# Attention projections in another order, one more convolution tap off VectorE, and another end of the kernel

## The chip, the cores and the metric

One core of one Trainium2 chip runs the kernel. The metric is device microseconds (us) of one execution. The engines are TensorE (PE in the rows; its weight loads are PEld), VectorE (DVE), ScalarE (ACT), GpSimd (POOL) and SyncE (SP), which here issues the DMAs.

## The reference

Two transformer-like blocks run one after the other on 512 tokens of width 1024, in fp32. The first block normalizes, projects, mixes the tokens with a state-space part and with a sparse attention, and ends with a feed-forward part. The second block mixes with two recurrent parts and ends with a convolutional feed-forward part and a final norm. What the change touches:

```python
h = rmsnorm(x, norm1_g)                          # first block
hp = h @ w_in                                    # q, the kv streams, gates
q = rmsnorm(q, q_norm_g)                         # each head's 64 values
kc = rmsnorm(compress_blocks(kv[0, 0], ...), k_norm_g[0])   # gelu(flat @ w1) @ w2
vc = compress_blocks(kv[0, 1], ...)
ks, kw = rmsnorm(kv[1, 0], ...), rmsnorm(kv[2, 0], ...)
...
u = dwconv2d(rmsnorm_mod(x) @ w_up, conv_w)      # second block: 3 x 3 taps on 8 x 64 tokens
a, b = split(u)
x = x + g2 * ((silu(a) * b) @ w_down)
out = rmsnorm(x, final_norm_w)
```

## The kernel before

Activations lie with channels on partitions and the 512 tokens along the free axis, in tiles of 128 channels. Every fp32 matrix product is done as three matmuls (`mm3`, lines 210 to 212): activation and weight are each split into a high part (rounded, "H", by ScalarE) and the rest ("L", a subtraction on VectorE or GpSimd), and high x high, low x high and high x low are summed in PSUM. A unit of weights is 128 output channels: `wload` brings it by DMA and splits it into one of three pairs of buffers `wh`, `wl`. `proj` goes through a list of units; a callback takes each finished PSUM tile. With `first=n` the first n units are computed together, with `tail=n` the last n in two halves of the tokens.

PSUM has eight banks, given out by `mmtile` under three tags: four "mm", three "aux" and one "sm". A tile must be read out before its bank is written again. The kernel is written on a layer that sets all the semaphores and that also orders the instructions of each engine: a planner simulates a timeline with costs of its own and takes, among the instructions that are ready in it, the one that comes first in the program. So program order is a priority, and each engine then runs its list in order.

**Attention projections** (`nsa_proj`, line 861). Eight units of `win` are taken in `order`: 4 and 5 are the streams that get compressed, 6 and 7 the keys of the other two branches, 0 to 3 the queries. Each key or query tile is scaled by the token's norm (`qk`, VectorE), squared (ScalarE), and two matmuls with a selector `hsel` (line 895, fp32, one pair for each tile) add the squares of each head into 12 rows of one PSUM tile that stays open through the six tiles. Then the 12 rows are copied, transposed, turned into inverse roots (`root`), transposed back, split (`r12`), and spread by a matmul for each tile (line 915); VectorE multiplies the tile, and `stack` (line 940) copies its halves to `qs` and `ks`. These take the place of the tiles hH and hL, the projections' input, so they can be written only when the last product of `nsa_proj`, the values and gates (`winv`, 96 matmuls into four "mm" tiles), has read it. `compress` (line 976) is a generator with small matmuls (line 1007 and following); after each unit from the third on, one piece of it is put into the program. In `nsa` (line 1075) the compressed values `vcz` enter by a matmul on 64 of the 128 rows (line 1143).

**Second feed-forward part** (`ffn2`, line 1998). `up` takes the units of `wup2`, two for each of 22 pairs. The first 18 units (9 pairs, `lead`) run without any other product, the first four together; then two units alternate with one unit of the down product. `conv_psum` (line 1649) does the nine taps on a unit's PSUM tile: the centre and the tap (-1, 0) on ScalarE, seven taps as multiply-adds on VectorE (line 200), and the addition of the (-1, 0) tap on GpSimd. `gate` multiplies a pair and splits it for the down product. From the fifth unit on GpSimd makes the low part of the weights.

**End.** The last eight units of the down product add to x. The final norm squares the eight tiles, adds them up on VectorE one after the other, sums over partitions by matmuls with ones (line 366), takes the power -1/2 on GpSimd, and spreads the factor (`rdg`, matmul at line 382). `store` makes each output tile with one VectorE instruction, and a DMA takes two tiles. It all runs for each half of the tokens. `between` puts the first half's outputs into the gaps of the second half's norm, in program order.

## Time and profile before

| | |
|---|---|
| runs, median (lowest to highest) | 1656.02 us (1654.74 to 1656.45) |
| profiled execution | 1655.87 us, span 1654.2 us |
| mean granted TensorE clock | 0.973 of full speed |
| busy, TensorE / VectorE / ScalarE / GpSimd | 1571.7 / 1155.2 / 733.0 / 399.6 us |

The span runs from the first to the last instruction. Busy time is the time in which an engine had an instruction in work; its share of the span is 95, 70, 44 and 24%.

### The profile page before, as it was taken

How to read it: one execution, taken by the hardware profiler on the slowest of the kernel's cores; microseconds unless marked ns; L12 is line 12 of the kernel's file. 1: busy time of each engine (PE TensorE's matmuls, PEld its weight loads, DVE VectorE, ACT ScalarE, POOL GpSimd, SP SyncE). 2: the span in 40 equal slices, each digit the busy share in tenths (PEclk: the TensorE clock that was granted, in tenths of full speed). 3: DMA queues.
4: the chain of work that ended last, by engine and by line, in shares of the span. 5: the costliest groups of instructions: out<-in, count | busy, mean ns of one | idle time of the engine just before them, and what ended most of it. 6: DMA issues, size and time to landing. Idle time of an engine off the chain costs nothing.

```text
span 1654.2 us, 22302 instructions
## 1 busy us (share of the span) xinstructions
PE 1571.7 (95%) x8277; PEld 1308.7 (79%) x8277; DVE 1155.2 (70%) x2209; ACT 733.0 (44%) x1286; POOL 399.6 (24%) x355
## 2 busy tenths in 40 slices
PE   7998898899999999999999999989989899999997
PEld 5887676677898888888887888878879788888886
DVE  8988625675769854863538888577868798777755
ACT  4354426553444213352335555556554454343422
POOL 1100203222100000000012222315220566656552
PEclk9999897999999999999999999999999899999998
DMA  5331310003346763733212011111212223233322
GB/s 178 105 96 47 124 59 26 14 20 98 126 166 206 249 218 110 250 124 102 83 64 65 26 39 52 59 52 51 77 52 69 72 94 102 90 102 91 101 86 80
DMA packets 60268, 158.34 MB, mean 96 GB/s; under 512 B 12416, under 2 KB 20352, under 8 KB 60032
## 3 DMA queue, kind: packets, MB, share of 16 engines
q1 hardware_dynamic: 60160, 156.92, 29.9%
q8 instruction: 65, 1.06, 0.3%
q14 instruction: 43, 0.35, 0.1%
HBM read 152.57 MB, written 2.10 MB: 94 GB/s over the span
## 4 chain that ended last, share of the span: by engine, by line
PE 73%; DVE 10%; ACT 5%; issue 2%; POOL 1%; DMA 0%; POOLq 0%; DVEq 0%; ACTq 0%
PE ps_mm L210 21%; PE ps_mm L211 21%; PE ps_mm L212 21%; PE ps_sm L1130 2%; PE ps_mm L1119 1%; DVE caccm L200 1%; DVE wl L191 1%; ACT L188 1%; DVE hgE L191 1%; PE ps_aux L1573 1%; DVE caccf L200 1%; PE ps_aux L1097 1%; ACT wh L188 0%; PE ps_mm L1007 0%; DVE hgl L1486 0%
## 5 line engine op out<-in xcount | busy, mean ns | idle before, releaser
L188 ACT ACTIVATE wh<-raw 128x1024 fp32r<-128x1024 f32 (+3 forms) x234 | 236.7, 1012 | 536.2 <-PE ps_mm L211 415.7
L191 DVE TENSOR_TENSOR wl<-raw,wh 128x1024 fp32r<-128x1024 f32 (+2 forms) x162 | 198.0, 1223 | 115.3 <-ACT wh L188 108.2
L200 DVE SCALAR_TENSOR_TENSOR caccf<-ps_mm,cwf,caccf 128x441 f32<-128x441 f32 (+2 forms) x308 | 206.7, 694 | 34.5 <-ACT ctapf L188 28.8
L191 POOL TENSOR_TENSOR wl<-raw,wh 128x1024 fp32r<-128x1024 f32 (+2 forms) x72 | 159.8, 2221 | 168.0 <-ACT wh L188 167.1
L210 PE MATMUL ps_mm<-h4H,wh 128*128 128x512 f32 (+1 forms) x368 | 137.0, 380 | 7.8 <-DVE caccf L200 7.6
L212 PE MATMUL ps_mm<-h4H,wl 128*128 128x512 f32 (+1 forms) x368 | 138.3, 378 | 0.0
L211 PE MATMUL ps_mm<-h4L,wh 128*128 128x512 f32 (+1 forms) x368 | 138.3, 379 | 0.0
L191 POOL TENSOR_TENSOR rr<-rv,nhalf 128x2 f32<-128x2 f32 x9 | 8.7, 968 | 435.0 <-DVE rv L197 435.0
L210 PE MATMUL ps_mm<-h2H,wh 128*128 128x512 f32 (+1 forms) x280 | 103.8, 372 | 0.0
L212 PE MATMUL ps_mm<-h2H,wl 128*128 128x512 f32 (+1 forms) x280 | 103.6, 371 | 0.0
L211 PE MATMUL ps_mm<-h2L,wh 128*128 128x512 f32 (+1 forms) x280 | 103.6, 371 | 0.0
L210 PE MATMUL ps_mm<-aH,wh 128*128 128x512 f32 (+1 forms) x272 | 102.6, 377 | 0.5 <-DVE x L191 0.5
L212 PE MATMUL ps_mm<-aH,wl 128*128 128x512 f32 (+1 forms) x272 | 102.7, 378 | 0.0
L211 PE MATMUL ps_mm<-aL,wh 128*128 128x512 f32 (+1 forms) x272 | 102.4, 377 | 0.0
L210 PE MATMUL ps_mm<-hH,wh 128*128 128x512 f32 x224 | 89.5, 406 | 9.6 <-ACT hH L188 8.9
L1265 DVE CUSTOM_DVE_ANT_0 msc<-wmod,cB,cols 128x1024 bf16<-128x1024 f32 x64 | 82.0, 1281 | 21.2 <-DMA wmod<-in_wmod 20.8
L211 PE MATMUL ps_mm<-hL,wh 128*128 128x512 f32 x224 | 90.1, 403 | 0.0
L212 PE MATMUL ps_mm<-hH,wl 128*128 128x512 f32 x224 | 89.4, 400 | 0.0
L210 PEld LDWEIGHTS ps_mm<-h4H,wh 128*128 128x128 f32 x368 | 68.7, 190 | 21.1 <-issue 7.7
L211 PEld LDWEIGHTS ps_mm<-h4L,wh 128*128 128x128 f32 x368 | 69.9, 190 | 13.2 <-DVE h4L L200 0.4
L212 PEld LDWEIGHTS ps_mm<-h4H,wl 128*128 128x128 f32 x368 | 69.8, 190 | 13.1
L210 PE MATMUL ps_mm<-faH,wh 128*128 128x512 f32 (+1 forms) x194 | 72.4, 373 | 0.0
(521 smaller groups left out, 4040.9 us busy)
## 6 DMA issues: line engine op xcount, KB each, us to landing
raw<-in_wup SPq DMA_DIRECT2D x76, 512.0 KB, 3.4
wmod<-in_wmod SPq DMA_DIRECT2D x48, 512.0 KB, 4.3
raw<-in_wdn SPq DMA_DIRECT2D x32, 512.0 KB, 3.5
raw<-in_win SPq DMA_DIRECT2D x28, 512.0 KB, 3.4
raw<-in_wout SPq DMA_DIRECT2D x8, 512.0 KB, 3.4
raw<-in_wdn2a SPq DMA_DIRECT2D x8, 512.0 KB, 3.4
raw<-in_wdn2b SPq DMA_DIRECT2D x8, 512.0 KB, 3.4
raw<-in_wdn2c SPq DMA_DIRECT2D x8, 384.0 KB, 3.0
```

The lines of the kernel that those rows point to most:

```text
L188: return self.nc.scalar.activation(o, i, f, **k)
L191: return (e or self.nc.vector).tensor_tensor(o, a, b, op)
L200: return self.nc.vector.scalar_tensor_tensor(o, a, s, b, op0, op1)
L210: mm(ps, wh, xh, start=start, stop=False)
L211: mm(ps, wh, xl, start=False, stop=False)
L212: mm(ps, wl, xh, start=False, stop=stop)
L1097: nc.tensor.matmul(S[:, :n2], self.qs[:, 2 * j + g, c], self.ks[:, 2 * br + g, :n2], start=True, stop=False)
L1119: nc.tensor.transpose(tp[:, 128 * b:128 * b + 128], P[g, i][:, 128 * b:128 * b + 128], self.ident)
L1130: nc.tensor.matmul(O[64 * g:64 * g + 64, 128 * i:128 * i + 128], self.V[:, b, c:c + 64], PT[g][:, 128 * b:128 * b + 128], start=br == 0 an ...
L1265: ins = nc.vector.tensor_tensor_reduce(sc, w, cB[:, c], 1.0, bm[:, m:m + 1], OP.mult, OP.add, acc)
L1573: nc.tensor.matmul(ps[:, j], EE[:, li, 128 * j:128 * j + 128], vw(EE[:, li])[:, j], start=True, stop=True)
```

## The change

The order of the eight attention units becomes 6, 7, 0, 1, 2, 3, 4, 5, and the compression comes into the program as one piece after the stacking, with its PSUM tiles under "aux". Squares are summed three tiles at a time: three selector matmuls write 32 rows each of one PSUM tile, given different column positions of the array; there are two such tiles, so eight transposes where there were four. `vcz` gets zeros in the rows not used, so that its matmul takes all 128 rows. In the feed-forward part the fifth and sixth unit take the banks "aux" and "sm", and the first 18 units have two taps on ScalarE and GpSimd; the taps' order changes. At the end the squares of tiles 0 to 4 are put into the program before the last three units, the eighth tile's squares go to the sum as a second matmul, tiles 6 and 7 of the output are made on ScalarE and GpSimd, and `between` goes away.

```diff
-             pre={}, mid0=None, mid_at=-2):
+             pre={}, mid0=None, mid_at=-2, banks=()):
...
-            ps = self.mmtile()
+            ps = self.mmtile(tag=banks[i - first] if i - first < len(banks) else "mm")
...
-    def sumsq(self, x, tmp, sl, tags=("nsq", "nacc")):
+    def sumsq(self, x, tmp, sl, tags=("nsq", "nacc"), tiles=range(8), acc=None):
         n = sl.stop - sl.start
-        acc = None
-        for k in range(8):
+        for k in tiles:
...
-    def rstd(self, acc, n, width, root=False, between=None):
+    def rstd(self, accs, n, width, root=False):
...
-            self.ss_turn = nc.tensor.matmul(ss[:, j:j + 1], acc[:, 128 * j:128 * j + 128], self.ones[:, :1], start=True,
-                                            stop=True).ins.name
-        between(2)
+            for i, acc in enumerate(accs):
+                self.ss_turn = nc.tensor.matmul(ss[:, j:j + 1], acc[:, 128 * j:128 * j + 128], self.ones[:, :1],
+                                                start=i == 0, stop=i == len(accs) - 1).ins.name
...
-        self.hsel = p.tile([128, 6, 12], F32, name="hsel")
+        self.hsel = p.tile([128, 32], F32, name="hsel")
         e.memset(self.hsel, 0.0)
+        for g in range(2):
+            e.memset(self.hsel[64 * g:64 * g + 64, g:g + 1], 1.0)
...
-        for a in range(6):
-            for g in range(2):
-                e.memset(self.hsel[64 * g:64 * g + 64, a, 2 * a + g:2 * a + g + 1], 1.0)
...
-        ss = self.mmtile((12, T), "aux")
+        slot = (4, 5, 0, 1, 2, 3)
+        sqs, s12 = [], []
...
-        order = (4, 5, 6, 7, 0, 1, 2, 3)
+        order = (6, 7, 0, 1, 2, 3, 4, 5)
...
         def out(i, ps, sl):
             unit(order[i], ps)
-            if i > 1:
-                next(cmp)
...
             self.tt(qk[a], ps, self.rb, OP.mult)
-            sq = qp.tile([128, T], F32, name="sq", tag="sq", bufs=1)
+            sp, tag, bufs = ((qp, "sq", 1), (p, "P03", 2), (p, "P03", 2))[slot.index(a) % 3]
+            sq = sp.tile([128, T], F32, name="sq", tag=tag, bufs=bufs)
             self.act(sq, qk[a], AF.Square)
-            nc.tensor.matmul(ss, self.hsel[:, a], sq, start=a == 4, stop=a == 3)
+            sqs.append(sq)
+            if len(sqs) == 3:
+                ss = self.mmtile((128, T), "aux")
+                for i in range(3):
+                    nc.tensor.matmul(ss[32 * i:32 * i + 32], self.hsel, sqs[i], start=True, stop=True,
+                                     tile_position=(0, 32 * i))
+                sp, tag, bufs = (p, "P03", 2) if s12 else (qp, "s12", 1)
+                t = sp.tile([96, T], F32, name="s12", tag=tag, bufs=bufs)
+                self.act(t, ss[:96])
+                s12.append(t)
+                sqs.clear()
...
-        s12 = qp.tile([12, T], F32, name="s12", tag="s12", bufs=1)
-        self.act(s12, ss)
-        tp = self.mmtile((128, 48), "aux")
-        for i in range(4):
-            nc.tensor.transpose(tp[:, 12 * i:12 * i + 12], s12[:, 128 * i:128 * i + 128], self.ident[:12, :12])
-        r = self.rsqrt(qp, tp, 48, 64, "rn")
+        rr = [qp.tile([128, 4, 2, 6], F32, name="rn" + x) for x in "vrt"]
+        for h in range(2):
+            tp = self.mmtile((128, 4, 3, 32), "aux")
+            for i in range(4):
+                nc.tensor.transpose(tp[:, i], s12[h][:, 128 * i:128 * i + 128], self.ident[:96, :96])
+            self.ts(rr[0][:, :, h].rearrange("p i (s g) -> p i s g", g=2), tp[:, :, :, 0:2], 1.0 / 64, OP.mult, EPS, OP.add)
+        rr = [x.rearrange("p i h s -> p (i h s)") for x in rr]
+        self.root(rr[1], rr[0], rr[2])
+        r = rr[1]
...
-            nc.tensor.matmul(rb, self.hselT[:, a], r12, start=True, stop=True)
+            nc.tensor.matmul(rb, self.hselT[:, slot.index(a)], r12, start=True, stop=True)
             self.stt(qk[a], qk[a], self.col(gcols[a]), rb, OP.mult, OP.mult)
             self.stack(a)
+
+        for _ in cmp:
+            pass
...
-        self.vcz = p.tile([128, 128], F32, name="vcz")
+        self.vcz = p.tile([128, 2, 128], F32, name="vcz")
...
-            hid = self.mmtile((64, 128), "mm")
+            hid = self.mmtile((64, 128), "aux")
...
-            rows = slice(64 * (j % 2), 64 * (j % 2) + 64)
-            nc.tensor.matmul(O, self.vcz[rows], PcT[j // 2][rows], start=False, stop=True, skip_group_check=True)
+            nc.tensor.matmul(O, self.vcz[:, j % 2], PcT[j // 2], start=False, stop=True, skip_group_check=True)
...
-    def conv_psum(self, ps, w, pool, tag, bufs, tbufs):
+    def conv_psum(self, ps, w, pool, tag, bufs, tbufs, n_pool):
...
-        t = pool.tile([128, T], F32, name="ctap" + tag, tag="ctap" + tag, bufs=tbufs)
...
         self.act(acc, ps, scale=w[:, 4:5])
-        self.act(tv[:, 0:7], rv[:, 0:7], scale=w[:, 1:2])
-        for dy, dx in ((1, 0), (0, -1), (0, 1), (-1, -1), (-1, 1), (1, -1), (1, 1)):
+        taps = ((0, -1), (0, 1), (-1, -1), (-1, 1), (1, -1), (1, 1), (1, 0), (-1, 0))
+        late = []
+        for i in range(8 - n_pool, 8):
+            dy, dx = taps[i]
+            c = 3 * (dy + 1) + dx + 1
+            iy = slice(max(0, dy), 8 - max(0, -dy))
+            t = pool.tile([128, T], F32, name="ctap" + tag, tag="ctap" + tag, bufs=tbufs)
+            self.act(g(t)[:, iy], rv[:, iy], scale=w[:, c:c + 1])
+            late.append((slice(max(0, -dy), 8 - max(0, dy)), g(t)[:, iy]))
+        for dy, dx in taps[:8 - n_pool]:
...
-        self.tt(av[:, 1:8], av[:, 1:8], tv[:, 0:7], OP.add, nc.gpsimd)
+        for oy, t in late:
+            self.tt(av[:, oy], av[:, oy], t, OP.add, nc.gpsimd)
...
-                conv[m] = self.conv_psum(ps, cw[:, m // 2 + 22 * (m % 2)], p, "f", 8, 6)
+                conv[m] = self.conv_psum(ps, cw[:, m // 2 + 22 * (m % 2)], p, "f", 8, 6, 2 if m < 2 * lead else 1)
...
             self.proj(I["wup2"][0:2 * lead], hs, up, first=4, pre={3: pre}, halves=True, le=[None] * 4 + [nc.gpsimd] * 18,
+                      banks=("aux", "sm"),
...
+            def factor(sl, acc):
+
+                acc = self.sumsq(self.x, p, sl, tiles=(5, 6), acc=acc)
+                sq = p.tile([128, 256], F32, name="nsq", tag="nsq", bufs=2)
+                self.act(sq, self.x[7][:, sl], AF.Square)
+                return self.rstd([acc, sq], 256, D)[0]
...
             def store(sl, rb):
-                for k in range(8):
-                    if k % 2 == 0:
-                        y = p.tile([128, 2, 256], F32, name="y", tag="faH", bufs=17)
-                    self.tc.keep_in_program_order(
-                        self.stt(y[:, k % 2], self.x[k][:, sl], fin[:, k:k + 1], rb, mul, mul))
-                    if k % 2:
-                        nc.sync.dma_start(self.out[k - 1:k + 1, :, sl].rearrange("k p n -> p k n"), y)
-                    yield
-
-            def between(n):
-                for _ in zip(range(n), s0):
-                    pass
-
-            rb = []
...
-            down("wdn2c", list(range(8)), 16, 6, tail=3, mid=lambda: rb.append(self.norm_factor(self.x, p, h0)))
-            s0 = store(h0, rb[0])
-            r1 = self.rstd(self.sumsq(self.x, p, h1), 256, D, between=between)[0]
-            for _ in store(h1, r1):
-                pass
+
+                y2 = p.tile([128, 2, 256], F32, name="y", tag="faH", bufs=17)
+                for i in range(2):
+                    self.act(y2[:, i], self.x[6 + i][:, sl], scale=fin[:, 6 + i:7 + i])
+                rbs = p.tile([128, 256], F32, name="rbl", tag="rbl", bufs=2)
+                self.act(rbs, rb)
+                for i in range(2):
+                    self.tt(y2[:, i], y2[:, i], rbs, mul, nc.gpsimd)
+                for k in range(0, 6, 2):
+                    y = p.tile([128, 2, 256], F32, name="y", tag="faH", bufs=17)
+                    for i in range(2):
+                        self.stt(y[:, i], self.x[k + i][:, sl], fin[:, k + i:k + i + 1], rb, mul, mul)
+                    nc.sync.dma_start(self.out[k:k + 2, :, sl].rearrange("k p n -> p k n"), y)
+                nc.sync.dma_start(self.out[6:8, :, sl].rearrange("k p n -> p k n"), y2)
+
+
+            early, rb = [], []
+
+            def mid():
+                rb.append(factor(h0, early[0]))
+
+            down("wdn2c", list(range(5)), 16, 6)
+            for i, sl in enumerate((h0, h1)):
+                early.append(self.sumsq(self.x, p, sl, tags=("nsq", f"nacc{i}"), tiles=range(5)))
+            down("wdn2c", [5, 6, 7], 16, 6, tail=3, mid=mid)
+            r1 = factor(h1, early[1])
+            store(h0, rb[0])
+            store(h1, r1)
```

## Rows read from the trace of the kernel before

**Rows 1.** Waits of TensorE, whole span: us in total, times, longest.

```profile
PE ps_mm L210 <- DVE caccf L200: 7.6, 1, 7.6
```

**Rows 2.** Busy time by stages: stretch, length; us busy (instructions) by engine; PEclk; DMA share, GB/s.

```profile
262.00:272.00 10.00, 5.76 (x15) 3.46 (x14) 9.66 (x19) 9.68 (x16) 2.06 (x3) 0.72 0.20 52
...
1286.00:1300.00 14.00, 6.44 (x46) 5.97 (x45) 11.77 (x19) 9.05 (x13) 8.25 (x4) 0.78 0.36 112
...
1304.00:1376.00 72.00, 72.00 (x319) 59.63 (x319) 64.63 (x103) 35.19 (x53) 46.47 (x27) 1.00 0.28 88
```

**Rows 3.** Timeline of TensorE, 1298 to 1305: start, us, instruction, count, idle before.

```profile
1298.49 0.76 PE L210 MATMUL ps_mm<-h4H,wh 128*128 128x512 f32 x1 [7.56 <-DVE caccf L200]
...
1304.11 0.39 PE L211 MATMUL ps_mm<-h4L,wh 128*128 128x512 f32 x1
1304.33 0.39 PE L212 MATMUL ps_mm<-h4H,wl 128*128 128x512 f32 x1
```

**Rows 4.** Timelines of VectorE and of GpSimd, same place.

```profile
1288.16 17.26 DVE L200 SCALAR_TENSOR_TENSOR caccf<-ps_mm,cwf,caccf 128x448 f32<-128x448 f32 x28 [5.75 <-ACT ctapf L188]
...
1287.10 4.75 POOL L191 TENSOR_TENSOR wl<-raw,wh 128x1024 fp32r<-128x1024 f32 x2 [14.87 <-ACT wh L188]
```

**Rows 5.** Groups by line, 1304 to 1376: count | busy us, mean ns | idle before.

```profile
L188 ACT ACTIVATE ctapf<-ps_mm,cwf 128x448 f32<-128x448 f32 x13 | 8.1, 625 | 0.0
...
L200 DVE SCALAR_TENSOR_TENSOR caccf<-ps_mm,cwf,caccf 128x441 f32<-128x441 f32 (+2 forms) x89 | 58.4, 692 | 7.4 <-ACT ctapf L188 6.4
...
L191 POOL TENSOR_TENSOR wl<-raw,wh 128x1024 fp32r<-128x1024 f32 x13 | 31.3, 2407 | 12.6 <-ACT wh L188 12.1
L191 POOL TENSOR_TENSOR caccf<-caccf,ctapf 128x448 f32<-128x448 f32 x14 | 16.2, 1156 | 15.9 <-DVE caccf L200 15.9
```

**Rows 6.** The page's 40 slices, TensorE: busy tenths.

```profile
PE   7998898899999999999999999989989899999997
```

**Rows 7.** Timeline of TensorE, attention: compression, one sum pair, and an attention product.

```profile
199.61 4.12 PE L1007 MATMUL ps_mm<-cw,cD 128*64 128x128 f32 x32
...
204.09 1.03 PE L895 MATMUL ps_aux<-sq,hsel 128*12 128x512 f32 x2
...
293.49 1.74 PE L1130 MATMUL ps_sm<-PT,V 128*64 128x128 f32 x26
```

**Rows 8.** Timelines of TensorE, VectorE and ScalarE, end of the projections.

```profile
257.24 0.29 PE L212 MATMUL ps_mm<-wh,hL 128*128 128x280 f32 x1
...
257.88 0.68 DVE L191 TENSOR_TENSOR r<-ps_aux,r 12x512 fp32r<-12x512 f32 x1 [4.40 <-ACT r L188]
...
254.81 0.48 ACT L188 ACTIVATE V<-ps_mm,rr 128x256 f32<-128x256 f32 x1 [0.16 <-PE ps_mm L212]
...
258.63 0.26 ACT L188 ACTIVATE gat<-ps_mm,rr 128x24 f32<-128x24 f32 x1
...
261.71 1.28 ACT L188 ACTIVATE qs<-qk 64x512 fp32r<-64x512 f32 x2 [0.93 <-DVE qk L200]
...
268.19 3.90 ACT L188 ACTIVATE qs<-qk 64x512 fp32r<-64x512 f32 x6
```

**Rows 9.** Timelines of ScalarE, TensorE, GpSimd and VectorE, end of the kernel.

```profile
1642.29 0.42 ACT L188 ACTIVATE nsq<-x 128x256 f32<-128x256 f32 x1 [0.42 <-DVE nacc L191]
...
1643.46 0.58 PE L366 MATMUL ps_sm<-ones,nacc 128*128 128x1 f32 x4 [1.63 <-DVE nacc L191]
...
1645.52 1.22 PE L382 MATMUL ps_aux<-rdg,ones 128*128 128x256 f32 x2 [1.49 <-DVE rdg L191]
...
1644.31 0.69 POOL L191 TENSOR_TENSOR rr<-rv,nhalf 128x2 f32<-128x2 f32 x1 [3.69 <-DVE rv L197]
...
1645.38 4.79 DVE L200 SCALAR_TENSOR_TENSOR y<-x,cols,ps_aux 128x256 f32<-128x256 f32 x12
```

**Rows 10.** Timelines of VectorE and GpSimd, before the end.

```profile
1617.14 1.64 DVE L191 TENSOR_TENSOR nacc<-nsq 128x256 f32<-128x256 f32 x1 [0.48 <-ACT nsq L188]
...
1616.65 1.85 POOL L191 TENSOR_TENSOR wl<-raw,wh 128x768 fp32r<-128x768 f32 x1 [2.27 <-ACT wh L188]
```

More of the change, by code (lines that the diff above doesn't have):

```diff
@@ L326, in norm_factor @@
     def norm_factor(self, x, tmp, sl):
-        return self.rstd(self.sumsq(x, tmp, sl), sl.stop - sl.start, D)[0]
+        return self.rstd([self.sumsq(x, tmp, sl)], sl.stop - sl.start, D)[0]
     def norm(self, x, g, h, tmp, shift, sl, tag="nt", rb=None, bufs=2):
@@ L355, in split_scaled @@
             self.stt(L[:, k, sl], x[k][:, sl], g[:, k:k + 1], H[:, k, sl].bitcast(F32), OP.mult, OP.subtract)
-    def rstd(self, acc, n, width, root=False, between=None):
+    def rstd(self, accs, n, width, root=False):
         nc = self.nc
-        pin = self.tc.keep_in_program_order if between else lambda i: i
-        between = between or (lambda n: None)
         nb = n // 128
@@ L365, in rstd @@
         for j in range(nb):
-            self.ss_turn = nc.tensor.matmul(ss[:, j:j + 1], acc[:, 128 * j:128 * j + 128], self.ones[:, :1], start=True,
-                                            stop=True).ins.name
-        between(2)
+            for i, acc in enumerate(accs):
+                self.ss_turn = nc.tensor.matmul(ss[:, j:j + 1], acc[:, 128 * j:128 * j + 128], self.ones[:, :1],
+                                                start=i == 0, stop=i == len(accs) - 1).ins.name
         v = self.sm.tile([128, 4], F32, name="rv", tag="rv", bufs=2)
-        pin(self.ts(v[:, :nb], ss[:, :nb], 1.0 / width, OP.mult, EPS, OP.add))
+        self.ts(v[:, :nb], ss[:, :nb], 1.0 / width, OP.mult, EPS, OP.add)
         r = self.sm.tile([128, 4], F32, name="rr", tag="rr", bufs=2)
@@ L377, in rstd @@
         dg = self.sm.tile([128, 512], F32, name="rdg", tag="rdg", bufs=1)
-        between(2)
-        pin(self.tt(dg[:, :n].rearrange("p (b t) -> p b t", b=nb), self.ident[:, None, :].to_broadcast([128, nb, 128]),
-                    r[:, :nb, None].to_broadcast([128, nb, 128]), OP.mult))
+        self.tt(dg[:, :n].rearrange("p (b t) -> p b t", b=nb), self.ident[:, None, :].to_broadcast([128, nb, 128]),
+                r[:, :nb, None].to_broadcast([128, nb, 128]), OP.mult)
         rb = self.mmtile((128, 512), "mm" if root else "aux")
         nc.tensor.matmul(rb[:, :n], self.ones, dg[:, :n], start=True, stop=True)
-        between(8)
         return rb[:, :n], r
@@ L602, in norm @@
         def norm():
-            r, self.rt = self.rstd(self.sumsq(xs, hp, full, ("yg", "glus")), T, D, root=True)
+            r, self.rt = self.rstd([self.sumsq(xs, hp, full, ("yg", "glus"))], T, D, root=True)
             self.act(self.rb, r)
@@ L958, in stack @@
             self.tt(L, t[r], H[r].bitcast(F32), OP.subtract, self.nc.gpsimd if a in (2,3) else None)
-    def rsqrt(self, p, ss, n, width, nm):
-        v, r, t = (p.tile([128, n], F32, name=nm + x) for x in "vrt")
-        self.ts(v, ss, 1.0 / width, OP.mult, EPS, OP.add)
-        self.root(r, v, t)
-        return r
     def root(self, r, v, t):
@@ L1013, in compress @@
         for m in (4, 5):
-            tp = self.mmtile((128, 64), "mm")
+            tp = self.mmtile((128, 64), "aux")
             nc.tensor.transpose(tp, hids[m - 4], self.ident[:64, :64])
@@ L1019, in compress @@
             yield
-        kp = self.mmtile((64, 64), "mm")
+        kp = self.mmtile((64, 64), "aux")
         nc.tensor.matmul(kp, hTs[0][:, 0], w2[:, :64], start=True, stop=True)
@@ L1031, in compress @@
         yield
-        vp = self.mmtile((128, 64), "mm")
+        vp = self.mmtile((128, 64), "aux")
         nc.tensor.matmul(vp, hTs[1].rearrange("p a b -> p (a b)"), w2[:, 64:], start=True, stop=True)
@@ L1035, in compress @@
             s = slice(32 * b, 32 * b + 32)
-            self.act(self.vcz[s, 64 * (b % 2):64 * (b % 2) + 64], vp[s])
-        tp = self.mmtile((128, 64), "mm")
+            self.act(self.vcz[s, b // 2, 64 * (b % 2):64 * (b % 2) + 64], vp[s])
+        tp = self.mmtile((128, 64), "aux")
         nc.tensor.transpose(tp, kz, self.ident[:64, :64])
@@ L1647, in conv @@
         return acc
-    def conv_psum(self, ps, w, pool, tag, bufs, tbufs):
+    def conv_psum(self, ps, w, pool, tag, bufs, tbufs, n_pool):
         nc = self.nc
         acc = pool.tile([128, T], F32, name="cacc" + tag, tag="cacc" + tag, bufs=bufs)
-        t = pool.tile([128, T], F32, name="ctap" + tag, tag="ctap" + tag, bufs=tbufs)
         g = lambda a: a.rearrange("p (y x) -> p y x", x=64)
-        av, rv, tv = g(acc), g(ps), g(t)
+        av, rv = g(acc), g(ps)
         self.act(acc, ps, scale=w[:, 4:5])
-        self.act(tv[:, 0:7], rv[:, 0:7], scale=w[:, 1:2])
-        for dy, dx in ((1, 0), (0, -1), (0, 1), (-1, -1), (-1, 1), (1, -1), (1, 1)):
+        taps = ((0, -1), (0, 1), (-1, -1), (-1, 1), (1, -1), (1, 1), (1, 0), (-1, 0))
[8 more added lines that the diff above has]
+        for dy, dx in taps[:8 - n_pool]:
             c = 3 * (dy + 1) + dx + 1
@@ L2063, in between @@
-            def between(n):
-                for _ in zip(range(n), s0):
-                    pass
-            rb = []
-            h0, h1 = slice(0, 256), slice(256, 512)
-            down("wdn2c", list(range(8)), 16, 6, tail=3, mid=lambda: rb.append(self.norm_factor(self.x, p, h0)))
-            s0 = store(h0, rb[0])
-            r1 = self.rstd(self.sumsq(self.x, p, h1), 256, D, between=between)[0]
-            for _ in store(h1, r1):
-                pass
+            h0, h1 = slice(0, 256), slice(256, 512)
```

## The prediction

> **What bounds the kernel now.** The share of busy time says TensorE, 95% (the table). What matters is the remaining 82.5 us of its span (1654.2 less 1571.7), so I read the waits of TensorE first. They are many and short; one of 7.6 us stands out, in the second feed-forward part, where the first matmul of a new unit waits for VectorE's convolution to give a PSUM bank back [rows 1]. Second, the table by stages: three stretches touched by the change have an idle TensorE, 1286 to 1300 (6.4 of 14 us busy, granted clock 0.78), 262 to 272 (5.8 of 10 us, clock 0.72) and the end; the stage from 1304 to 1376, between, has TensorE busy for all of its 72 us [rows 2]. Third, the timeline of each of the three, since a gain counts only if TensorE is dense from there to the next stop. The time compared is the profiled execution's 1655.87 us: 1654.2 of span and 1.67 around it, which I leave as it is. The median of the runs, 1656.02, is 0.01% away, so no correction.
>
> **Feed-forward, start.** The first four units are computed together and hold all four "mm" banks. TensorE stands for 7.56 us until 1298.49, and then it runs slowly: thirteen matmuls from 1298.49 to 1304.11 take 5.62 us, where the pitch of the next pieces is 0.22 to 0.23 (1304.11 to 1304.33), 2.95 us for thirteen [rows 3]. That is 2.67 us for the low clock level (1.2 GHz; 2.4 is the other), which follows the idle time. The change gives the fifth and sixth unit the banks "aux" and "sm". A unit is 8 x 3 matmuls, 24 x 0.227 = 5.44 us, so TensorE has 10.9 us of work from about 1290.9 to 1301.8 before it asks for an "mm" bank. Are the weights there? Two units' low halves leave GpSimd from 1287.10 to 1291.85, one as 1290.9 is reached, the other with 4 us to spare [rows 4]. Is the first bank back by 1301.8? In the trace it came at 1298.49, inside 28 convolution taps that VectorE runs in 17.26 us from 1288.16 [rows 4]; with 24 taps they end at 1288.16 + 24 x 0.616 = 1302.9, the first unit's before that. So the stall goes with its clock: 7.56 + 2.67 = **10.2 us**. Bounds: 10.2 and, if the planner interleaves the taps so that the first unit's end among the last at 1302.9, or the second's are later still, about 5.
>
> What is late next? One tap more per unit for the first 18 units goes to ScalarE (0.625 us) and GpSimd (1.156), and VectorE loses one of 0.69 [rows 5]. These 18 units are dense on TensorE at 5.5 us a unit (13 units in 72 us) [rows 2, 5]. VectorE was at 64.63 of 72, 4.97 a unit; it falls to 4.3. That is worth nothing in itself, since it was not the limit from 1304 on. ScalarE goes from 2.7 to 3.3 a unit, off the path. GpSimd goes from 46.47 of 72, 3.6 a unit, to 2.407 + 2 x 1.156 = 4.72, still below 5.44: cost 0, hidden under the matmuls, with 0.7 us a unit to spare. Behind a GpSimd addition that waits for its taps stands the split of a later unit's weights, and TensorE waits for that; if the cover goes, the price is the last rival. For later units only the order of the taps is changed: 0. From 1304 TensorE's slices stay at 9 tenths or more to the last but one [rows 6], so the 10.2 reaches the end.
>
> **Projections.** From the glu on, TensorE is dense until the last V matmul starts at 257.24 [rows 8]. In that stretch six pairs of sum-of-squares matmuls take 1.03 us each, about 1.1 with the matmul behind, which starts slower [rows 7]: 6.6. The new ones are two groups of three pairs on 32 columns each. Side by side a group is about 1.03, one after the other 3.1, and I find nothing that puts a group beyond these two. The nearest row: 26 half-width instructions of 128 columns in 1.74 us, 0.067 each, against 32 of full output layout, 4.12 us, 0.129 each [rows 7]: neighbours on different columns run nearly twice as fast, so I take 1.1 a group, 2.2 together; saved 4.4 (0.4 if serial). Added ahead of the last V matmul: six broadcasts of the factors, which ran after it, 6 x 0.227 = 1.4; four more transposes and one more interruption, about 0.7. Net 2.3: the V products end at 255.2 instead of 257.5. The compression's matmuls, two runs of 4.12, stay ahead of that end (they come before V in the program): moved, not removed, 0.
>
> After them the old order waits: the factors are split on VectorE at 257.88, the scaling follows, and the first copy to the stacked heads on ScalarE at 261.71 [rows 8]. The copies need scaled q and k and the h tiles free (the stacked tiles take their place). With q and k first, the scaling is over during the last two units, so the copies start when h is free, 255.4: 6.3 us earlier. From there ScalarE is the path: 16 copies until 272.09, then a table load and the exponentials [rows 8]. What is late next is ScalarE itself: the evacuations of V and the gates, 254.81 to 258.89, lay in its idle time [rows 8] and now partly fall into the copies. They start 2.7 us before the end of V (257.5), so up to 1.4 are left; I take 0.8. The memsets of the stacked keys on GpSimd and the compression's small ScalarE work move with the same wait for h, or lie beside the 12 us of V matmuls: 0. Sum **5.5 us**. Bounds: the norm's transposes and broadcasts now stand inside the running units on TensorE's in-order queue, and behind each of them a unit's matmuls; if their inputs come late by a microsecond or two at each of four places, the gain is gone: -1. The other end is 14 (first rival). The zero-padded V of the compressed branch keeps 512 streamed columns: 0. SP's loads of compression weights move back by six units, behind the unit weights that are needed first: 0.
>
> **The end.** Old chain after the last residual: the last square waits 0.42 for a buffer (1642.29), an addition follows, TensorE sums from 1643.46, GpSimd's power is 1644.31 to 1645.00, the factor's broadcast is 1645.52 to 1646.74, and VectorE has twelve products left at 1645.38, to 1650.17, 0.40 each, eight of them behind the broadcast [rows 9]. New: no buffer wait and no last addition, less two more sums, about 0.5 earlier; six products behind the broadcast instead of eight, 0.8; the other two go to ScalarE and GpSimd beside them. Sum **1.3 us**; 0.5 to 2.5.
>
> One row speaks against the new GpSimd products: an addition of two SBUF tiles on VectorE took 1.64 us beside a GpSimd product that ran 1616.65 to 1618.50, where twelve products of the same 256 columns run at 0.40 each [rows 9, 10]. The Trainium skill (GPSIMD Engine Reference, Specifications) says that GpSimd shares its SBUF interfaces with VectorE, in contention with instructions that have two SBUF inputs. The trace agrees. By it, the diagonal of the second half's factor (two SBUF inputs) can be held by a product of the first half, up to 0.7 us, and the end would give 0.6 instead of 1.3.
>
> Together 10.2 + 5.5 + 1.3 = 17.0: 1655.87 - 17.0 = **1638.9 us**.
>
> **Rivals.** (1) The compression's 8.2 us of matmuls fall behind V, into the time when TensorE waits for ScalarE's copies, and h is free 8.2 earlier. For it: TensorE has 4.2 us idle from 262 to 272 [rows 2] and the matmuls no longer use the "mm" banks that V holds. Against: in program order they stand before V and their inputs are ready early in V's 12 us. 1655.87 - 25.2 = 1630.7.
> (2) The start gives half: the fifth and sixth units run at once, but the banks come late, as the 24 taps end at 1302.9 and not at 1301.8, and each stop brings slow matmuls; 5 for the start and 2 for the projections, 1.3 for the end: 1647.6.
> (3) It doesn't do what it says: the planner's order puts new stops into the units (norm) and the start, and nothing or 3 us remain: 1653 to 1657.
> (4) GpSimd's queue becomes the bound of the first 18 units. It had 28.5 us of waits in those 72 us, 2.2 a unit, for ScalarE's copies and for VectorE's taps in turn [rows 5]. With 4.72 of work, and the waits as long as now, a unit takes 6.9 and TensorE follows it through three weight buffers: 1.46 x 14 units (the fifth to the eighteenth) = 20.5 lost, 1659.4, slower. It decides from 17.0 / 14 = 1.2 us a unit. Against: most of those waits are slack of an engine that is early, and VectorE ends its taps sooner.
>
> **Numbers.** Forecast 0.53, (1) 0.12, (2) 0.20, (3) 0.08, (4) 0.07. The forecast's own range is 1634 to 1644; towards (1) the low end is 1630, and to hold most of (2) the high end is 1650, which leaves out (3), (4) and a little of (1). This kernel's time can be told from no change at about 0.2%, 3.3 us: faster is the first three, 0.85; the same 0.08; slower 0.07.
>
> **What would show it.** Start: the wait for a convolution's bank is gone, the stretch 1291 to 1304 (shifted) is busy at full clock, and no wait of TensorE for weights comes in the units after. Projections: the six-instruction groups take about 1 us, the V products end 2.3 us earlier, the first copy starts within 1 us of them, the exponentials 5 to 6 us earlier. End: the last product about 1.3 us nearer to the last matmul. Wrong would be a new TensorE wait in the units, or the first unit's taps ending after TensorE asks.

## The result, and the profile after

The changed kernel takes 1637.19 us (median of 4 runs, 1636.85 to 1637.37) against 1656.13 for the kernel before on the same chip: ratio 0.9887, 95% interval 0.987 to 0.9904, 18.9 us less. The prediction was 1638.9, 17.0 less. The total came out nearly as forecast; its three terms did not.

To see the terms, I cut every trace at five marks on TensorE: **A**, the first product of `ysH` behind the wait of 7.49 us for ScalarE; the first product of `mH` (the merge behind the attention); the first of `h4H` (second feed-forward part); the first of `faH`; the last of `faH`/`faL`. The table holds the start of A and the differences of the starts, in us, with the kernels of the experiments below; each row is one execution. "Stretch 1" is projections and attention, "stretch 3" the first feed-forward units.

| kernel | A | 1: to `mH` | 2: to `h4H` | 3: to `faH` | 4: to last | to end | span |
|---|---|---|---|---|---|---|---|
| before | 175.92 | 239.56 | 850.30 | 122.42 | 252.92 | 13.08 | 1654.2 |
| changed | 175.06 | 229.88 | 849.96 | 113.79 | 253.36 | 12.75 | 1634.8 |
| changed, again (e9) | 175.06 | 229.63 | 849.95 | 113.73 | 253.37 | 12.76 | 1634.5 |
| e1 banks | 173.65 | 238.67 | 852.32 | 121.46 | 252.92 | 12.98 | 1652.0 |
| e2 taps | 175.88 | 240.10 | 849.62 | 119.09 | 252.92 | 13.09 | 1650.7 |
| e5 banks and taps | 177.77 | 240.24 | 849.50 | 113.75 | 252.91 | 13.03 | 1647.2 |
| e3 projections | 174.57 | 230.25 | 849.97 | 122.48 | 252.92 | 12.41 | 1642.6 |
| e4 end | 174.83 | 241.21 | 849.59 | 122.45 | 253.36 | 13.46 | 1654.9 |
| e6 sums adjacent | 176.34 | 226.82 | 850.19 | 113.73 | 253.36 | 12.76 | 1633.2 |
| e7 compression early | 173.22 | 227.21 | 848.93 | 113.74 | 253.37 | 12.63 | 1629.1 |
| e8 compression late | 175.56 | 244.81 | 849.03 | 113.76 | 253.37 | 13.37 | 1649.9 |
| e10 end ordered | 177.74 | 229.80 | 850.07 | 113.72 | 253.37 | 12.20 | 1636.9 |
| e11 adjacent, early | 175.35 | 224.15 | 849.42 | 113.78 | 253.37 | 12.63 | 1628.7 |
| e12 all | 175.15 | 226.74 | 849.32 | 113.76 | 253.37 | 12.06 | 1630.4 |

Stretch 3 repeats to 0.1 us between kernels with the same code there. Stretch 1 spreads by 2.5 over the five kernels that have the old projections (238.67 to 241.21, mean 239.96) and by 0.6 over the four with the new ones as changed (229.63 to 230.25, mean 229.89). So the change gives 10.1 in the projections (predicted 5.5), 8.7 in the feed-forward start (122.45 to 113.75; predicted 10.2), and takes 0.4 in stretch 4, with nothing sure from there to the end (12.41 to 13.09 with the old end, 12.63 to 13.46 with the changed one; predicted gain 1.3).

Stages of the changed kernel, which answer to [rows 2] (it runs ahead by some 11 us at the feed-forward part):

```profile
250.00:262.00 12.00, 8.56 (x57) 7.90 (x58) 9.59 (x9) 9.97 (x18) 9.05 (x7) 0.87 0.46 131
262.00:272.00 10.00, 8.24 (x32) 7.02 (x31) 3.51 (x16) 6.27 (x21) 3.31 (x4) 0.50 0.00 0
1275.00:1288.00 13.00, 12.27 (x74) 10.64 (x73) 10.08 (x17) 9.97 (x15) 9.15 (x5) 1.00 0.33 105
1288.00:1300.00 12.00, 12.00 (x54) 9.95 (x53) 6.79 (x12) 6.85 (x11) 12.00 (x9) 1.00 0.30 107
1300.00:1372.00 72.00, 71.63 (x316) 58.91 (x315) 67.98 (x107) 45.17 (x72) 64.86 (x43) 1.00 0.30 95
```

The hole at the feed-forward start is closed, at granted clock 1.00. GpSimd rises to 64.86 of 72 and TensorE is still busy for 71.63. TensorE's waits there, against the 7.6 of [rows 1]:

```profile
PE ps_sm L212 <- POOL wl L191: 0.7, 1, 0.7
PE ps_mm L210 <- DVE caccf L200: 0.4, 1, 0.4
```

Timeline of TensorE around the end of the projections, for [rows 7, 8] (start, us, instruction, idle before). L895 are the sums, L1012 the compression, L1020 and L1043 its transposes, L1102 the first score:

```profile
198.85 1.04 PE L895 MATMUL ps_aux<-sq,hsel 128*32 128x512 f32 x2
...
218.75 1.05 PE L895 MATMUL ps_aux<-sq,hsel 128*32 128x512 f32 x4
...
250.42 4.13 PE L1012 MATMUL ps_aux<-cw,cD 128*64 128x128 f32 x32 [0.57 <-DVE qk L200]
...
259.99 0.36 PE L1020 MATMUL ps_aux<-ident,chs 64*128 64x64 f32 x1 [2.48 <-ACT chs L188]
...
267.16 0.34 PE L1043 MATMUL ps_aux<-ident,kz 64*128 64x64 f32 x1 [1.40 <-DVE kz L200]
267.42 0.58 PE L1102 MATMUL ps_aux<-ks,qs 128*128 128x256 f32 x1
```

ScalarE there: the first copy to the stacked heads, the last group of them, and the first exponential.

```profile
246.41 1.29 ACT L188 ACTIVATE qs<-qk 64x512 fp32r<-64x512 f32 x2
...
254.47 3.88 ACT L188 ACTIVATE qs<-qk 64x512 fp32r<-64x512 f32 x6
...
269.06 0.40 ACT L188 ACTIVATE P<-P,mn 128x128 f32<-128x128 f32 x1
```

The V products end at 246.39 (257.53 before), the compression now follows them, and the sums stand in five places of the units, not two. The end, against [rows 9]: VectorE runs six products of the first half ahead of the second half's variance `rv`, and the last six start behind ScalarE's copy.

```profile
1623.22 2.44 DVE L200 SCALAR_TENSOR_TENSOR y<-x,cols,ps_aux 128x256 f32<-128x256 f32 x6 [0.36 <-ACT rbl L188]
1625.57 0.15 DVE L197 TENSOR_SCALAR rv<-ps_sm 128x2 f32<-128x2 f32 x1
1626.53 0.42 DVE L191 TENSOR_TENSOR rdg<-ident,rr 128x256 f32<-128x256 f32 x1 [0.81 <-POOL rr L191]
1628.16 2.44 DVE L200 SCALAR_TENSOR_TENSOR y<-x,cols,ps_aux 128x256 f32<-128x256 f32 x6 [1.21 <-ACT rbl L188]
```

### The profile page after: what moved, and what is told of

Its sections match the earlier page's. It is cut to its first block, busy times and chain, and to the rows that moved or that the text cites. A ratio compares the mean times of both kernels' runs of the same rounds, so it can differ in the third digit from the quotient of the medians.

```text
span 1634.8 us, 22321 instructions
## 1 busy us (share of the span) xinstructions
PE 1557.2 (95%) x8289; PEld 1302.4 (80%) x8289; DVE 1144.3 (70%) x2186; ACT 745.0 (46%) x1311; POOL 423.7 (26%) x367
## 3 DMA queue, kind: packets, MB, share of 16 engines
q8 instruction: 65, 1.06, 0.3%
## 4 chain that ended last, share of the span: by engine, by line
PE 72%; DVE 10%; ACT 5%; issue 2%; POOL 1%; DMA 0%; DVEq 0%; ACTq 0%
PE ps_mm L210 20%; PE ps_mm L212 20%; PE ps_mm L211 20%; PE ps_sm L1135 2%; DVE wl L191 1%; PE ps_mm L1124 1%; DVE caccm L200 1%; ACT L188 1%; DVE hgE L191 1%; PE ps_aux L1102 1%; ACT wh L188 1%; PE ps_aux L1104 1%; PE ps_aux L1577 1%; DVE caccf L200 1%; DVE hgl L1490 0%
## 5 line engine op out<-in xcount | busy, mean ns | idle before, releaser
L200 DVE SCALAR_TENSOR_TENSOR caccf<-ps_mm,cwf,caccf 128x441 f32<-128x441 f32 (+2 forms) x278 | 188.5, 695 | 30.9 <-ACT ctapf L188 24.7
L212 PE MATMUL ps_mm<-h4H,wl 128*128 128x512 f32 (+1 forms) x352 | 131.2, 375 | 0.0
L211 PE MATMUL ps_mm<-h4L,wh 128*128 128x512 f32 (+1 forms) x352 | 131.1, 375 | 0.0
L210 PE MATMUL ps_mm<-h4H,wh 128*128 128x512 f32 (+1 forms) x352 | 129.7, 377 | 0.6 <-DVE caccf L200 0.4
L211 PEld LDWEIGHTS ps_mm<-h4L,wh 128*128 128x128 f32 x352 | 66.2, 188 | 12.5 <-DVE h4L L200 0.4
L212 PEld LDWEIGHTS ps_mm<-h4H,wl 128*128 128x128 f32 x352 | 66.2, 188 | 12.2
L210 PEld LDWEIGHTS ps_mm<-h4H,wh 128*128 128x128 f32 x352 | 65.0, 188 | 13.3 <-issue 0.8
```

Source lines behind the costliest of these rows:

```text
L200: return self.nc.vector.scalar_tensor_tensor(o, a, s, b, op0, op1)
L210: mm(ps, wh, xh, start=start, stop=False)
L211: mm(ps, wh, xl, start=False, stop=False)
L212: mm(ps, wl, xh, start=False, stop=stop)
```

## The experiments

**Each part alone on the kernel before (e1 to e4), then two together (e5).** Each is the kernel before with only those lines of the diff. e1:

```diff
+                      banks=("aux", "sm"),
```

> One part alone on the kernel before: the fifth and sixth feed-forward units get the banks "aux" and "sm"; the taps stay at 28 in VectorE for the first four units. The prediction's sizes: the stall of 7.56 us and the slow matmuls of 2.67 us go together, but the taps end later than with 24, 28 x 0.616 = 17.26 us after their start, at the time when TensorE asks for an "mm" bank, so 6 to 10 us gained, 1646 to 1650. Theory B, from the trace of the changed kernel (its feed-forward stretch is 8.4 us shorter and keeps 0.73 and 0.37 us of waits): the banks are all of it, 7 to 9 us, 1647 to 1649. Theory C, the banks only move the stall behind the sixth unit because the taps set the pace: under 4 us, 1652 or more.

Measured: 1653.81 us, ratio 0.9998 (0.9989 to 1.0008); stretch 3 is 121.46, 1.0 less. Theory C. TensorE's waits from 1270 to 1400 (us in total, times, longest):

```profile
PE ps_mm L210 <- DVE caccf L200: 6.2, 2, 4.9
```

and the second of the two stops in TensorE's timeline:

```profile
1329.72 0.76 PE L210 MATMUL ps_mm<-h4H,wh 128*128 128x512 f32 x1 [4.88 <-DVE caccf L200]
```

The stop of [rows 3] is not removed; most of it moves 31 us on, and slow matmuls follow it again (granted clock 0.82 from 1330 to 1340). VectorE is busy for all of the 10 us ahead of it. e2:

```diff
-                conv[m] = self.conv_psum(ps, cw[:, m // 2 + 22 * (m % 2)], p, "f", 8, 6)
+                conv[m] = self.conv_psum(ps, cw[:, m // 2 + 22 * (m % 2)], p, "f", 8, 6, 2 if m < 2 * lead else 1)
```

> One part alone on the kernel before: a second tap of the first 18 units on ScalarE and GpSimd, and the new order of taps; no new banks, projections and end as before. The prediction's price of this part is 0 where TensorE is dense; alone, where the stall is still there, four taps fewer in VectorE before the first bank is free bring 0.6 to 2.5 us: 1653.5 to 1655.5. The rival that GpSimd's queue becomes the bound of these units: 1.2 us a unit or more, 1670 or so.

Measured: 1652.12, ratio 0.998 (0.9971 to 0.9989), stretch 3 3.3 less. The one wait for a bank falls from 7.6 to this:

```profile
PE ps_mm L210 <- DVE caccf L200: 4.0, 1, 4.0
```

1.4 us more than the expected bounds, and no sign of GpSimd as the bound. e5, both:

> The two feed-forward parts together on the kernel before (new banks, and the second tap of the first 18 units off VectorE); projections and end as before. Alone they gave 0.4 to 1.7 us (banks) and 3.4 us (taps). Theory A, the two add up: 1651 to 1652. Theory B, each lacks the other: with the banks alone the stall of 7.56 us only moves, to 4.9 us some 31 us later, because VectorE gains on TensorE too slowly to give the banks back in time; with fewer taps it does. Then both together bring the 8.4 us that the feed-forward stretch of the changed kernel is shorter: 1646 to 1648.

Measured: 1647.11, ratio 0.9947 (0.9932 to 0.9963), stretch 3 113.75: 8.7 less, where the parts alone sum to 4.3. Theory B: the banks let TensorE go on, and only the shorter taps keep VectorE's backlog from stopping it again.

e3, the projections alone:

```diff
-        order = (4, 5, 6, 7, 0, 1, 2, 3)
+        order = (6, 7, 0, 1, 2, 3, 4, 5)
```

> One part alone on the kernel before: the projections (keys and queries first, compressed streams last, sums of squares in two groups, compression in "aux" banks, zero-padded V of the compressed branch). Prediction: 5.5 us, 1650.6. Theory B, from the trace of the changed kernel, where the attention starts 10 us sooner and the compression's matmuls lie behind the V products: 10 to 11 us, 1645 to 1646, with the stretch of the glu ahead of it 0.9 us shorter.

Measured: 1642.79, ratio 0.9929 (0.9914 to 0.9943); stretch 1 230.25, 9.7 under the mean of the old ones. By the stage, theory B's size; the median is 12.7 under the kernel before's (1655.5), more than either theory (four runs, 1641.15 to 1644.53). The part of theory B on the glu fell, since A differs as much between kernels with one order there. e4, the end alone:

```diff
-            r1 = self.rstd(self.sumsq(self.x, p, h1), 256, D, between=between)[0]
+            r1 = factor(h1, early[1])
+            store(h0, rb[0])
+            store(h1, r1)
```

> One part alone on the kernel before: the end (first five tiles' squares summed earlier, last square straight into TensorE's sum, two of eight products on ScalarE and GpSimd, no order pinned between the two halves). Prediction: 1.3 us, 1654.8, bounds 0.5 to 2.5. Theory B, from the trace of the changed kernel (12.5 us from the last matmul of the residuals to the end, 12.8 before): 0.3 us, 1655.8, because six products of the first half run on VectorE ahead of the second half's factor.

Measured: 1656.86, ratio 1.0009 (0.9999 to 1.0018): no gain, at most a loss. Stretch 4 is 0.44 longer, as in every kernel with the new end; the trace shows eight one-column sums of the first half inside it, where the old end had four; no run changes these alone.

**Sums adjacent (e6)**, on the changed kernel:

```diff
-            self.act(sq, qk[a], AF.Square)
+            last = self.act(sq, qk[a], AF.Square).ins.name
...
+                    if i < 2:
+                        self.tc.add_manual_dep(ins.ins, last, NOSYNC, reason="group")
```

> The changed kernel, but the first two sums of squares of each group are ordered behind the third square, so that the three of a group follow one another on TensorE (in the changed kernel five interruptions of 1.04 to 1.05 us hold the six). The prediction's step (side by side a group of three takes about 1.05 us): two interruptions instead of five, 3.1 us sooner at the last V matmul, and 2 to 3 us in all, 1634 to 1635. The rival, that they run one after the other however they are placed: the group takes 3.1 us, no gain, 1637; the factors come some microseconds later, which could cost up to 1: 1638.

Measured: 1632.32, ratio 0.9861 (0.9845 to 0.9877), a little more gain than expected; stretch 1 226.82, 3.1 less. Timeline of TensorE:

```profile
205.57 1.06 PE L895 MATMUL ps_aux<-sq,hsel 128*32 128x512 f32 x6
...
223.12 1.06 PE L895 MATMUL ps_aux<-sq,hsel 128*32 128x512 f32 x6
```

Six instructions on three column groups take 1.06 us, two on one took 1.04. The prediction's price for a group was right; the changed kernel's order does not make the groups.

**Compression ahead of the end of V (e7)**, the place that the prediction gave it; all its PSUM tiles go to "sm", of which the cut shows one:

```diff
         self.proj([I["win"][4 + m] for m in order], hs, out)
+        for _ in cmp:
+            pass
...
-            hid = self.mmtile((64, 128), "aux")
+            hid = self.mmtile((64, 128), "sm")
```

> The changed kernel, but the compression is traced directly behind the units (in bank "sm"), so that its matmuls fall ahead of the end of the V products, as the prediction had it. Theory A, that the compression fell behind V is what made the gain in the attention larger than predicted: V ends 8 to 9 us later (255), and the time is 4 to 5 us longer, 1641 to 1642. Theory B, the order of the compression only decides where the wait lies: the copies end 8 us later but the exponentials follow them directly (267 to 268.5, against 269.06), and the time stays at 1636 to 1638.

Measured: 1632.97, ratio 0.9862 (0.9845 to 0.9878). Both theories expected too long a time: stretch 1 is 227.21, 2.7 less than the changed kernel's. V ends at 254.73, the first copy is at 254.70, the last copy ends at 264.96 and the first exponential is here:

```profile
267.70 0.40 ACT L188 ACTIVATE P<-P,mn 128x128 f32<-128x128 f32 x1
```

From A that is 94.48 us, against 94.00 in the changed kernel (269.06 less 175.06): no gain up to there. The gain lies behind it. TensorE's waits, changed kernel from 190 to 420:

```profile
PE ps_aux L1142 <- DVE cX L191: 4.8, 1, 4.8
PE ps_aux L1020 <- ACT chs L188: 2.8, 2, 2.5
PE ps_aux L1043 <- DVE kz L200: 1.4, 1, 1.4
PE ps_aux L1102 <- DVE mn L1108: 1.1, 3, 0.5
```

and with the compression early:

```profile
PE ps_aux L1102 <- DVE mn L1108: 4.6, 6, 2.0
PE ps_sm L1043 <- ACT vcz L188: 2.4, 1, 2.4
PE ps_aux L1102 <- ACT ks L188: 1.3, 2, 0.9
...
PE ps_aux L1060 <- ACT kcbd L188: 0.8, 1, 0.8
```

The wait for `cX` (the compressed branch's weights, in TensorE's queue ahead of the second branch) is gone; so is the one for the gelu. The kernel before has the wait for `cX` too:

```profile
PE ps_aux L1137 <- DVE cX L191: 4.8, 1, 4.8
```

From 285 to 305 TensorE is busy for 18.70 of 20 us, against 15.19 (A is 1.84 earlier in e7; from 283.16 to 303.16, as far behind A as the other, it is 18.70 too).

**Compression after the first branch (e8):**

```diff
                 if j == 0 and br == 1:
+                    for _ in self.cmp:
+                        pass
                     X = self.nsa_cmp(p)
```

> The changed kernel, but the compression is traced after the first branch of the first head pair, directly ahead of its use. Theory A, the chain through the compression (gelu behind ScalarE's 16 copies, 10.7 us from the last copy at 258.35 to the first exponential at 269.06) bounds the start of the attention: the first exponential comes at 259.7 to 261, two more table loads cost 2.6, and 3 to 6 us are gained, 1631 to 1634. Theory B, behind the first exponentials the same work of ScalarE and VectorE has to be done, and the compression's matmuls and table loads now stand in it: no gain or a loss of up to 3, 1637 to 1640.

Measured: 1652.29, ratio 0.9987 (0.9972 to 1.0001): 15 us slower than the changed kernel, worse than either theory, though the first exponential came at 260.30. TensorE's waits:

```profile
PE ps_mm L1125 <- DVE P L196: 7.7, 4, 4.5
PE ps_aux L1103 <- DVE mn L1109: 5.4, 7, 3.3
PE ps_aux L1011 <- DMA cw<-in_ck: 2.1, 2, 1.1
```

From 262 to 285 VectorE is busy for 6.26 us and ScalarE for 7.29 of 23: the compression's chain stands alone there, its weights loaded late into buffers that it shares with the attention. Being first at the exponentials is worth nothing by itself.

**The changed kernel again (e9, no edit), and the end in another order (e10):**

```diff
-            r1 = factor(h1, early[1])
-            store(h0, rb[0])
-            store(h1, r1)
+            s0 = store(h0, rb[0][0])
...
+            r1 = factor(h1, early[1], between, "mm")
...
+            rc = self.mmtile((128, 512), copy)
+            nc.tensor.matmul(rc[:, :n], self.ones, dg[:, :n], start=True, stop=True)
```

> The changed kernel itself, beside the three below on the same chip, so that differences of a few microseconds between them can be read. Both theories: 1637, ratio to the kernel before 0.9887 within its interval.

> The changed kernel with another order at the end: the second half's variance and diagonal on VectorE go ahead of four of the first half's six products, GpSimd's power ahead of its products, and the broadcast factor is written to a second bank that ScalarE reads, so that VectorE need not wait for ScalarE's copy. Theory A, the end gave nothing because of the two stops in VectorE (the variance 1.1 us late behind six products, then 1.21 us behind ScalarE's copy): 1.5 to 2.3 us less than the changed kernel. Theory B, the chain of square, sum, power, diagonal and broadcast with the write to memory sets the end, whatever VectorE does beside it: 0 to 0.7 us less.

Measured: e9 1636.35, ratio 0.9882 (0.9863 to 0.9902); e10 1636.70, 0.9883 (0.9865 to 0.9901). Theory B. VectorE's two stops are gone:

```profile
1626.94 0.86 DVE L200 SCALAR_TENSOR_TENSOR y<-x,cols,ps_aux 128x256 f32<-128x256 f32 x2
1627.84 0.94 DVE L191 TENSOR_TENSOR rdg<-ident,rr 128x256 f32<-128x256 f32 x1
1628.70 3.31 DVE L200 SCALAR_TENSOR_TENSOR y<-x,cols,ps_aux 128x256 f32<-128x256 f32 x8
```

The last product ends 7.31 us behind the last `fa` start (1632.01 less 1624.70), against 8.55 in the changed kernel (1630.60 less 1622.05), but the kernel's end comes only 0.55 sooner (12.20, 12.75). The rest goes into writing: what the DMA engines moved in 40 slices from 1618 to 1660, first changed, then e10:

```profile
GB/s 0 0 0 0 0 0 95 342 341 220 0 201 338 350 110 0 8 8 0 0 0 0 0 0 0 0 0 0 0 0 0 0 0 0 0 0 0 0 0 0
```

```profile
GB/s 0 0 0 0 0 0 0 0 55 195 248 32 343 344 331 351 99 0 8 8 0 0 0 0 0 0 0 0 0 0 0 0 0 0 0 0 0 0 0 0
```

Eight transfers of 256 KB at 330 to 350 GB/s; with the first half's products later, more of them crowd behind the last.

**Together (e11), and with a transposition moved and the new end (e12).** e12's own edit traces the transposed `kz` ahead of the `vp` product.

> The changed kernel with the sums of squares adjacent and the compression ahead of the end of the V products. Alone the spans were 1.6 and 5.7 us shorter than the changed kernel's. Theory A, the two add up (one moves the end of V, the other what follows it): span 1627 to 1628. Theory B, behind V both work on the same wait (first exponentials), and the smaller is lost: span 1629.

> The two together, with the new order at the end, and with the transposed compressed key traced ahead of the compressed value (with the compression early TensorE waited 2.42 us for its bank, held until ScalarE had copied the compressed value, and 0.83 us for its copy). Theory A: both waits go and the end gives 1.5 to 2.3 us, span 1623 to 1625. Theory B, only what bounds the first exponentials counts, ScalarE's copies: 0 to 1 for the transposition and 0 to 0.7 for the end, span 1626.5 to 1628.

Measured: e11 1630.43, ratio 0.9845 (0.9829 to 0.986), span 1628.7. It is the fastest, on one chip with e9 5.9 us under it. In stretch 1 the two add up: 224.15, 5.7 under the 229.89, where e6 gave 3.1 and e7 2.7 (theory A; in the spans the unequal A hides it). e12 1633.24, 0.9863: slower than e11. Both theories fell. TensorE's waits from 228 to 420:

```profile
PE ps_aux L1113 <- DVE mn L1119: 4.1, 5, 2.8
PE ps_aux L1153 <- DVE w L1124: 3.0, 1, 3.0
PE ps_sm L1052 <- ACT kcbd L188: 1.8, 1, 1.8
```

The wait of 2.4 is shortened to 1.8, and the stop ahead of the `cX` transposes (L1153) is back with 3.0. VectorE ends the last product with `cX` at 292.82 in e12 and at 288.70 in e11, where it follows its inputs directly. In e12 two score operations, the biases of the next heads and a product `gt` that waits for TensorE are ahead of it in VectorE's queue, and then it takes 2.26 us instead of 1.23. e12's VectorE and GpSimd:

```profile
289.95 0.69 DVE L191 TENSOR_TENSOR gt<-gt,ps_mm 128x512 f32<-128x512 f32 x1 [0.47 <-PE ps_mm L212]
290.56 2.26 DVE L191 TENSOR_TENSOR cX<-cX,csm 128x1024 f32<-128x1024 f32 x1
...
290.47 1.26 POOL L191 TENSOR_TENSOR wl<-raw,wh 128x512 fp32r<-128x512 f32 x1 [6.27 <-ACT wh L188]
```

So a small edit ahead of it changed the order in VectorE's queue, and with it more than the edit itself was worth.

## Why the prediction was right in sum, and wrong in its terms

**Feed-forward start, predicted 10.2 for the banks and 0 for the taps; 8.7 for both.** The stall went, with its slow matmuls, as said; 0.73 and 0.37 us of waits remain, and 0.4 is not assigned. The step that failed is the price of the taps: "That is worth nothing in itself, since it was not the limit from 1304 on." It was not the limit while TensorE stood 10 us behind. VectorE at 4.97 a unit against 5.44 makes up 0.5 a unit, and with the stall taken away by the banks its backlog meets TensorE once more (e1: 4.88 at 1329.72). Nor did VectorE fall to 4.3 a unit: in the changed kernel it is busy for 67.98 of the 72 us (64.63 before), since it works off the backlog, 91 taps where 13 units have 78. The banks and the taps are one gain: 1.0 and 3.3 alone, 8.7 together. GpSimd stayed under its limit, 64.86 of 72, so rival 4 did not come.

**Projections, predicted 5.5; 10.1.** Three steps failed. The events of stretch 1, in us from A of each kernel:

| from A to | before | changed | e7 | e11 |
|---|---|---|---|---|
| end of V | 81.61 | 71.33 | 81.51 | 78.35 |
| first copy | 85.79 | 71.35 | 81.48 | 78.32 |
| first exponential | 97.48 | 94.00 | 94.48 | 91.33 |
| first product with V | 108.74 | 102.17 | 107.37 | 104.22 |
| merge (`mH`) | 239.56 | 229.88 | 227.21 | 224.15 |

The sums: side by side was right (1.06 for a group, e6), but only one pair of pairs met in the changed kernel. Five interruptions of 1.1 instead of six save 1.1 and not 4.4; e6 gives 3.1 of it back. (The row of [rows 7] that the prediction took for full output layout has 64 columns, as the other has; the conclusion drawn from it came true all the same.)

"The compression's matmuls ... stay ahead of that end (they come before V in the program): moved, not removed, 0": they fell behind it, which is the mechanism of rival 1, and V ended 10.3 sooner, not 2.3. In the queue they stand behind the broadcasts of the factors, the last two of which run from 249.21.

But rival 1's price was wrong too. The copies start 14.4 sooner, the exponentials 3.5: the gelu waits behind 16 copies on ScalarE, and the scores behind the compression on TensorE.

With the order that was predicted (e7), the times on the clock look as worked out (V's end 254.73 for 255.2, the first copy 254.70 for 255.4), but only because A comes 2.7 earlier in e7's execution. From A they are 0.1 and 4.3 sooner than before, not 2.3 and 6.3, and the exponentials 3.0, not 5.5: the sums are still scattered. With the sums adjacent as well (e11) it is 3.3, 7.5 and 6.2, so up to the exponentials the working holds within 1.2.

And yet stretch 1 is 12.8 under the mean of the old kernels in e7, and 15.8 in e11. So the third failure decides: the sum ended at the exponentials, as if all behind them moved along. In the changed kernel 3.5 there became 6.6 at the first product with V and 9.7 at the merge. TensorE runs the first scores in one piece (267.42 to 272.48), where before waits drew them out from 264.51 to 275.77. Its granted clock is 0.99 from 272.5 to 276.5, and before 0.50 from 276 to 285, so the 32 small products with `kcbd` behind the scores took 3.82 us instead of 6.92 (before, then changed):

```profile
275.57 6.92 PE L1055 MATMUL ps_aux<-kcbd,qk 128*128 128x64 f32 x32
...
272.28 3.82 PE L1060 MATMUL ps_aux<-kcbd,qk 128*128 128x64 f32 x32
```

TensorE over stretch 1 (length, us busy, granted clock, DMA share, GB/s): before, changed, e7, e11.

```profile
175.92:415.48 239.56, 225.70 (x1254) 0.93 0.20 61
...
175.06:404.94 229.88, 216.59 (x1259) 0.95 0.21 64
...
173.22:400.43 227.21, 216.34 (x1259) 0.94 0.21 64
...
175.35:399.50 224.15, 213.30 (x1259) 0.94 0.21 65
```

It is idle for 13.9 us before and 13.3 in the changed kernel (13.9 to 15.0 in the five kernels with the old projections, 13.3 to 14.7 in the four with the new ones). So the 10.1 are not waits that went: TensorE waits as long as before and needs less time for its work. The sums are 1.1 of that. The clock, 0.93 against 0.95, is 5.3 by an estimate from these rows (0.07 x 239.56 less 0.05 x 229.88; e9 has 0.97 at the same length, so it is rough). The zero padding, priced at 0, shows 0.15 to 0.2 at each of four places (from the first product with `vcz` to the third matmul behind the second, 315.73 to 317.36 before and 306.32 to 307.74). The rest is not assigned. In e7 and e11, where the wait for `cX` is gone, the idle time is 10.9.

**End, predicted 1.3; no gain, and 0.4 lost in stretch 4.** The price of six products behind the broadcast for eight (0.8) was spent: the variance waited 1.1 behind six products of the first half, and the last products started only behind ScalarE's copy, 0.45 after the broadcast had ended at 1627.71 (of the 1.21 that VectorE was idle, 0.76 went by before that). That both are not the whole is e10's result: without them the last product is 1.24 sooner, and the writes give back more than half. The Trainium skill (GPSIMD Engine Reference, Specifications) has GpSimd share its SBUF interfaces with VectorE, in contention with instructions that have two SBUF inputs, as the diagonal has. In the changed kernel the diagonal took 0.42, not held; in e10, beside two GpSimd products from 1627.77 to 1629.36, it took 0.94. The trace of e10 agrees; the changed kernel's loss had other causes.

8.7 + 10.1 - 0.4 = 18.4, of the 18.9 measured; errors of -1.5, +4.6 and -1.7 met in a total that was off by 1.9. That it came so near is luck.

Open: the time to A differs by up to 4.6 us (173.22 to 177.77). Between the kernel before, e1 and e5, whose TensorE order is the same there, it is 173.65 to 177.77; the first product waits 8.4 to 10.3 us for its input in them, and the rest was not traced. That stretch 1 gains from the lost wait for `cX` in e7 and e11 is read from their traces and from its return in e12; no run changed that wait alone. Nor was the order of the units or the zero padding run alone, so the 10.1 is shown for the projections as a whole and not for its parts.

## What to carry to other kernels

A stall that one engine causes in another may only move when there is more room (here, banks), and go when the causing engine has less to do as well, so try such parts alone and together. A stretch can get shorter though TensorE waits as long as before: look at busy time and granted clock, not at waits alone. Where a planner orders the queues, a place in the program is no place in the queue, and a gain must be followed past the first milestone to the next dense stretch. Compare stages between marks, not spans, and count events from a mark, not from the start of the trace, when the differences are a few microseconds.

## What the runs showed that I had not expected

Matmuls on three column groups run fully side by side: 1.06 us for six instructions, 1.04 for two. VectorE's operations with two SBUF inputs stretch beside GpSimd's: the diagonal 0.94 for 0.42 (e10), the product with `cX` 2.26 for 1.23 (e12), and in the changed kernel two low halves of the keys 3.29 (at 253.03) where two of the queries took 1.40 (at 247.07). The last 2.1 MB are written at about 340 GB/s, and e10 shows that rate taking back half of what the arithmetic gained.
